# TensorE's and VectorE's order written out in the first stage of a two-layer encoder kernel, and the input's high part taken straight from x

## The chip, the cores and the metric

The kernel runs on one core of a Trainium2 chip. The metric is the device time of one execution in microseconds; the time before is the median of three executions.

## The reference

Two layers over a sequence of 512 tokens of width 1024, batch 1, in float32. Layer 0 mixes tokens by stick-breaking attention with 16 heads, layer 1 by a gated token-mixing MLP; each mixer is followed by a SwiGLU feed-forward part. Every part has an adaptive norm in front, and the change is in the first of these and the projections behind it:

```python
shift, scale, gate = jnp.split(silu(c) @ w_ada + b_ada, 3, axis=-1)
h = rms_norm(x, g) * (1.0 + scale) + shift          # (512, 1024)
qkv = h @ w_qkv                                     # (512, 3072)
...                                                 # attention on q, k, v
x = x + gate * rms_norm(y, post_g)
```

## The kernel before

All matmuls that carry the result run as three products of float32r parts: a tensor is split into a high part (a rounding copy on ScalarE) and a low part (its difference on VectorE), and `mm3` issues high x high, high x low and low x high. Weight tiles of 512 KB stream through `wload` (the load, two raw buffers) and `wemit` (the split `wh`, `wl`, five buffers); `wget` asks for a tile and may run ahead.

The first stage normalizes x (`norm0`), transposes it to eight column blocks `xhT` of 128 features by 512 tokens (`turn0`), and needs per feature a scale `Ac = (1 + scale) * g` and a shift `Bc`, as columns. The adaLN product for them is taken in five blocks: for features 0 to 255 in two rows (`row0`, on TensorE), for the rest in three blocks of 512 columns (`ada0_sum`): eight multiply-add steps on VectorE (`ada_stt`) into `acc`, then four one-column matmuls (`cols0`, output `ab`) that sum over the partitions. `h0` forms `Ac` and `Bc` on VectorE, scales `xhT` in place on ScalarE, and splits it into `hTh` and `hTl`. A step k of the projections uses one column block: `v_step` has 12 matmuls into four banks (first half of v), `qk0_step` has 6 into `pq` and `pk` (first pair of heads). Blocks b = 1, 2, 3 of the adaLN columns belong to k = 2 and 3, 4 and 5, 6 and 7.

Behind it come the second half of v, the attention with the other q and k projections between its parts (`fill`), and the adaLN gate of layer 0 (`Bg`: VectorE steps `G`, `A`, `B` over loads `rawada`, summed over partitions by matmuls with `ones` into a bank that the attention scores call z).

A scheduler puts the instructions in each engine's queue, in order of their readiness by its own costs. Where a chain is on (`pe["chain"]`, `Vector.chain`), TensorE's or VectorE's instructions keep the order in which the program writes them. Before, both chains are off in the first stage and come on in the attention. Loads are issued by SP in one queue, at most eight in flight before it waits for an earlier one to land. ScalarE has no chain.

Of the kernel before, what the change touches and what calls it, by code (L numbers as in the profile page):

```python
# [31 lines left out]
def trunk(ctx: ExitStack, tc: tile.TileContext, A: dict, out: bass.AP):  # L32
    nc = tc.nc

    consts = ctx.enter_context(tc.tile_pool(name="consts", bufs=1))
    wraw = ctx.enter_context(tc.tile_pool(name="wraw", bufs=2))
    wpool = ctx.enter_context(tc.tile_pool(name="wpool", bufs=5))
    adas = ctx.enter_context(tc.tile_pool(name="adas", bufs=1))
# [10 lines left out]
    def nm(s):  # L49
        uid[0] += 1  # L50
        return f"{s}_{uid[0]}"
# [4 lines left out]
    def bank(name, tag="b"):  # L56
        return psum.tile([P, 512], F32, tag=tag, bufs=6 if tag == "b" else 2, name=nm(name))

    act = nc.scalar
    pe = {"prev": None, "chain": False}  # L60

    class Vector:


        chain, prev = False, None

        def __getattr__(self, op):
            def call(*args, **kw):
# [16 lines left out]
    def order(b, before):  # L85
        tc.add_manual_dep(
            b.ins, before.ins.name,
            mybir.DependencyInfo(mybir.DependencyClass.NoSync, mybir.DependencyReason.DATA),
            reason="order",
        )  # L90

    def mm(o, l, r, start, stop, after=None):
        b = nc.tensor.matmul(o, l, r, start=start, stop=stop, skip_group_check=True)  # L93
        pe_op(b)
        if after is not None:
            order(b, after)
# [15 lines left out]
    def split(hi, lo, src, hi_dve=False):  # L112
        if hi_dve:
            dve.tensor_copy(hi, src)
        else:
            act.activation(hi, src, AF.Copy)  # L116
        dve.tensor_tensor(lo, src, hi.bitcast(F32), ALU.subtract)
# [19 lines left out]
    def wemit():  # L137
        n = len(got)
        src, a, b, key = stream[n]
        if len(raws) == n:  # L140
            wload()
        if src is None:
            if len(raws) == n + 1 < len(stream) and stream[n + 1][0] is None:
                wload()
            got.append(blocks(*raws[n]))
            return
        raw = raws[n]
        if key[0] == "wdn" and key[2] in SEVEN[key[1]]:
            got.append(down_blocks(raw))
            return  # L150
        h, l = wtile(a, b)
        if key[0] == "wqk" and key[1]:

            act.activation(h[:], raw[:], AF.Copy)
            nc.vector.tensor_tensor(l[:], raw[:], h[:].bitcast(F32), ALU.subtract)
            if len(raws) == n + 1 and stream[n + 1][3][0] == "wqk":
                wload()
        else:
            act.activation(h[:], raw[:], AF.Copy)  # L159
            nc.vector.tensor_tensor(l[:], raw[:], h[:].bitcast(F32), ALU.subtract)  # L160
        got.append((h, l))

    def wtile(a, b):
# [121 lines left out]
    def ada0_raw(b, q):  # L285

        nk, n = (4, 256) if b < 2 else (2, 512)
        raw = stp.tile([P, nk, n], F32, tag="ra", bufs=8, name=nm("ada0"))
        load(raw[:], A["ada0s"][b, q] if b < 2 else A["ada0p"][b - 2, q])
        return raw  # L290

# [37 lines left out]
    class Bg:  # L329
# [79 lines left out]
    def hTk(hT, k, lo, n):  # L409
        h, l = hT[k // 2]  # L410
        return h[:, k % 2, lo : lo + n], l[:, k % 2, lo : lo + n]
# [162 lines left out]
        bg.step(bg0.step(n))  # L574


    b1 = consts.tile([P, KD], F32, name="b1")
    dve.tensor_scalar(b1[:], cols[:, 0, :], 1.0, None, ALU.add)

    xhT = [slot(F32, "xhT") for _ in range(4)]  # L580

# [37 lines left out]

    onec = oneb[:, 0:1]  # L620

    def ada0_sum(raws, n, nk, tag="acch"):
        acc = adas.tile([P, 512], F32, tag=tag, name=nm("acc"))
        nc.gpsimd.memset(acc[:, :n], 0.0)
        for q, raw in enumerate(raws):
            for k in range(nk):
                ada_stt(acc[:, :n], raw[:, k, :], q * nk + k)
        return acc

    def cols0(acc, n):  # L630

        ps = bank("ab0", "p")
        for i in range(n):
            mm(ps[:, i : i + 1], acc[:, i * P : (i + 1) * P], onec, True, True)
        return ps

    def row0(raws):

        ps = bank("ab0", "p")
        for q, raw in enumerate(raws):  # L640
# [3 lines left out]
        dve.tensor_copy(row[0:1, :], ps[0:1, :256])  # L644
        ps = bank("ab0", "p")
        for i in range(2):
            mm(ps[:, i : i + 1], row[0:1, i * P : (i + 1) * P], oneb[0:1, 0:1], True, True)
        return ps

    def h0(ps, i, k):  # L650

        Ac = small.tile([P, 1], F32, tag="Ac", name=nm("Ac"))
        Bc = small.tile([P, 1], F32, tag="Bc", name=nm("Bc"))
        dve.tensor_scalar(
            Ac[:], ps[:, i : i + 1], b1[:, k : k + 1], cols[:, 2, k : k + 1], ALU.add, ALU.mult
        )
        dve.tensor_scalar(Bc[:], ps[:, i + 1 : i + 2], cols[:, 1, k : k + 1], None, ALU.add)
        xk = xhT[k // 2][:, k % 2, :]
        act.activation(xk, xk, AF.Identity, scale=Ac[:], bias=Bc[:])
# [11 lines left out]
    norm0(1)  # L671
    turn0(0)
    norm0(2)
    ab0 = row0(a0)
    turn0(1)
    norm0(3)
    turn0(2)
    turn0(3)
    wv0.append(wget(("wv", 0, 0), 0))
    a2 = [ada0_raw(2, q) for q in range(4)]  # L680
    h0(ab0, 0, 0)
    ab1 = row0(a1)
    wqk0.append(wget(("wqk", 0, 0), 0))
    vb = [bank("v0") for _ in range(NT)]
    pq0, pk0 = bank("pq"), bank("pk")
    v_step(vb, 0, 0, wv0[0])
    h0(ab1, 0, 1)
    wqk0.append(wget(("wqk", 0, 1), 0))
    wload()
    acc = ada0_sum(a2, 512, 2)  # L690
    for b in range(1, 4):

        if b > 1:
            v_step(vb, 0, 2 * b - 2, wv0[b - 1])
        qk0_step(2 * b - 2)
        an = [ada0_raw(b + 2, q) for q in range(4)] if b < 3 else []
        if b == 1:
            v_step(vb, 0, 1, wv0[0])
        ps = cols0(acc, 4)
        h0(ps, 0, 2 * b)  # L700
        wv0.append(wget(("wv", 0, b), 0))
        h0(ps, 2, 2 * b + 1)
        if b < 3:
            wload()
            acc = ada0_sum(an, 512, 2, ("acch", "accl")[b % 2])
        if b > 1:
            v_step(vb, 0, 2 * b - 1, wv0[b - 1])
        if b == 2:
            bg0.step(3)
        qk0_step(2 * b - 1)  # L710
        if b == 3:
            bg0.step(1)
    for k in (6, 7):
        v_step(vb, 0, k, wv0[3])
        bg0.step(1)
        qk0_step(k)
        bg0.step(1)
# [758 lines left out]
```

## Time and profile before

| | us |
|---|---|
| median of three executions | 1159.36 (1157.38 to 1160.34) |
| the profiled execution, whole | 1159.46 |
| its span, first to last instruction | 1157.7 |
| mean granted TensorE clock | 0.996 |

Times in the views count from the span's start. In rows of instructions the first number is the start and the second the duration; in brackets stands the engine's idle time before it and what ended it. PE is TensorE, DVE VectorE, ACT ScalarE, POOL GpSimd, SP SyncE, which issues the loads. A 128x512 row of `v` is one matmul of the first stage. Lines are those of the kernel before; most rows carry the line of a helper (L93 is `mm`, L69 is `Vector`, L116 is `split`).

### The profile page before, as it was taken

To read this page: it belongs to the slowest core of one execution; us is meant where nothing else is said; L and a number is where in the kernel's file an instruction comes from. 1 tells how busy PE (TensorE), PEld (TensorE's weight loads), DVE (VectorE), ACT (ScalarE), POOL (GpSimd) and SP (SyncE) were. 2 spreads that over 40 slices of the span, in tenths; PEclk is the share of its full clock that TensorE was granted. 3 is DMA by queue.
4 is the path that set the end of the run, shared out by engine and by line. 5 is a ranking of instruction groups with operands and counts; after the bars stand their busy time and mean duration, and the time that the engine had idled before them with its cause. 6 is when DMAs were issued, how large, how long until landed. Compare 5 with 4: busy or idle time off the path is not lost.

```text
span 1157.7 us, 18780 instructions
## 1 busy us (share of the span) xinstructions
PE 1133.7 (98%) x7526; PEld 1011.6 (87%) x7526; DVE 943.4 (81%) x1220; ACT 587.6 (51%) x977; POOL 23.8 (2%) x43
## 2 busy tenths in 40 slices
PE   6999999999999999999999999999999999999997
PEld 4777888878999999998887898988999999999996
DVE  4987999875998998878686965668979898889996
ACT  6344454555665555554142633526545555565752
POOL 0020000000000000000000100000000000000000
PEclk9999999999999999999999999999999999999999
DMA  8764334213424444338887374224243433223242
GB/s 310 279 240 158 128 110 128 91 56 127 162 93 142 137 141 137 121 114 276 279 279 246 135 248 170 91 74 164 93 145 128 159 132 127 78 90 97 89 149 104
DMA packets 50811, 174.43 MB, mean 151 GB/s; under 512 B 5786, under 2 KB 9114, under 8 KB 50724
## 3 DMA queue, kind: packets, MB, share of 16 engines
q1 hardware_dynamic: 48996, 166.94, 42.6%
q0 software_dynamic: 1728, 6.29, 1.4%
q8 instruction: 59, 0.97, 0.3%
q14 instruction: 28, 0.23, 0.1%
HBM read 164.82 MB, written 8.39 MB: 150 GB/s over the span
## 4 chain that ended last, share of the span: by engine, by line
PE 87%; DVE 5%; DMA 3%; ACT 2%; issue 1%; SPq 0%; DVEq 0%; ACTq 0%
PE r L93 31%; PE y L93 15%; PE pqk L93 7%; PE v L93 6%; PE gu L93 5%; PE X L93 4%; PE Y L93 3%; PE u L93 3%; PE av L93 3%; PE z L93 2%; PE Z L93 1%; PE W L93 1%; PE tw L101 1%; PE tp L101 1%; PE ab L93 1%
## 5 line engine op out<-in xcount | busy, mean ns | idle before, releaser
L93 PE MATMUL r<-Sh,wl 128*128 128x256 f32 x608 | 170.3, 280 | 0.0
L93 PE MATMUL r<-Sh,wh 128*128 128x256 f32 x608 | 170.1, 280 | 0.0
L93 PE MATMUL r<-Sl,wh 128*128 128x256 f32 x608 | 170.0, 280 | 0.0
L93 PE MATMUL y<-wh,as 128*128 128x512 f32 x480 | 153.1, 396 | 0.4 <-DVE G L69 0.4
L159 ACT ACTIVATE wh<-raw 128x1024 fp32r<-128x1024 f32 x87 | 91.6, 1058 | 115.2 <-PE y L93 62.1
L69 DVE TENSOR_TENSOR wl<-f,wh 128x1024 fp32r<-128x1024 f32 x87 | 106.1, 1219 | 38.9 <-ACT wh L116 38.8
L116 ACT ACTIVATE wh<-f 128x1024 fp32r<-128x1024 f32 x87 | 92.3, 1061 | 89.0 <-PE r L93 66.2
L160 DVE TENSOR_TENSOR wl<-raw,wh 128x1024 fp32r<-128x1024 f32 x87 | 105.7, 1219 | 38.6 <-ACT wh L159 38.3
L93 PEld LDWEIGHTS r<-Sh,wh 128*128 128x128 f32 x608 | 114.6, 189 | 0.2 <-ACT e L1033 0.2
L93 PEld LDWEIGHTS r<-Sl,wh 128*128 128x128 f32 x608 | 114.5, 188 | 0.0
L93 PEld LDWEIGHTS r<-Sh,wl 128*128 128x128 f32 x608 | 114.5, 188 | 0.0
L93 PEld LDWEIGHTS y<-wh,as 128*128 128x128 f32 x480 | 90.1, 188 | 21.7 <-DVE G L69 0.8
L93 PE MATMUL y<-wl,as 128*128 128x512 f32 x240 | 94.9, 395 | 0.0
L93 PE MATMUL r<-hTh,wh 128*128 128x256 f32 x304 | 89.1, 293 | 0.3 <-DVE gu L69 0.2
L93 PE MATMUL r<-hTl,wh 128*128 128x256 f32 x304 | 84.9, 280 | 0.0
L93 PE MATMUL r<-hTh,wl 128*128 128x256 f32 x304 | 80.1, 280 | 0.0
L93 PEld LDWEIGHTS r<-hTh,wh 128*128 128x128 f32 x304 | 57.2, 188 | 6.1 <-DVE gu L69 1.9
L93 PE MATMUL r<-hTh,b 128*128 128x256 f32 x304 | 60.7, 282 | 0.0
L93 PEld LDWEIGHTS r<-hTl,wh 128*128 128x128 f32 x304 | 57.4, 189 | 0.1
L116 ACT ACTIVATE wh<-rawx 128x1024 fp32r<-128x1024 f32 x38 | 40.4, 1062 | 32.3 <-PE r L93 30.9
L93 PE MATMUL v<-wh,hTh 128*128 128x512 f32 x128 | 52.2, 408 | 3.1 <-ACT hTh L116 3.1
L93 PEld LDWEIGHTS r<-hTh,wl 128*128 128x128 f32 x304 | 55.2, 189 | 0.0
(261 smaller groups left out, 3023.8 us busy)
## 6 DMA issues: line engine op xcount, KB each, us to landing
rawada<-in_ada SPq DMA_DIRECT2D x80, 512.0 KB, 4.6
rawy<-in_wy SPq DMA_DIRECT2D x38, 512.0 KB, 3.5
rawx<-in_wx SPq DMA_DIRECT2D x38, 512.0 KB, 4.4
raw<-in_wdown SPq DMA_DIRECT2D x22, 512.0 KB, 4.5
raw<-in_wdn SPq DMA_DIRECT2D x22, 512.0 KB, 3.6
raw<-in_wqk SPq DMA_DIRECT2D x16, 512.0 KB, 4.5
ada<-in_ada0p SPq DMA_DIRECT2D x12, 512.0 KB, 6.0
raw<-in_wgu SPq DMA_DIRECT2D x12, 512.0 KB, 3.6
```

The lines of the kernel that those rows point to most:

```text
L69: b = getattr(nc.vector, op)(*args, **kw)
L93: b = nc.tensor.matmul(o, l, r, start=start, stop=stop, skip_group_check=True)
L101: last_tp[0] = nc.tensor.transpose(o, i, ident)
L116: act.activation(hi, src, AF.Copy)
L159: act.activation(h[:], raw[:], AF.Copy)
L160: nc.vector.tensor_tensor(l[:], raw[:], h[:].bitcast(F32), ALU.subtract)
```

## The change

- TensorE's and VectorE's chains are on from the first h step to the end of the first half of v, and weight tiles split in that time put their low part into VectorE's chain too (`dve.weights`). ScalarE's two activations of `h0` keep their order among themselves; its weight passes are left to the scheduler.
- The steps are written in another order: `v_two` issues the eight matmuls with h's high part first and the four with its low part last; the column sums (`sums0`) stand ahead of the q and k matmuls of the block's last k; the eight `ada_stt` steps are dealt out between the low parts (`Sum0.step`).
- `h0` computes h's high part from x in one scaled activation, then x itself by a second one; the low part is their difference.
- The constants (1 + bias, bias) enter the column sums as one more matmul with the identity (`cols0`), and one VectorE multiplication gives scale and shift of two k.
- Eleven buffers instead of eight for the adaLN loads of the stage; two of the second block's four loads are issued ahead of a weight tile's.
- The adaLN gate's steps in the stage are placed anew (3, 1, 1, then 3 instead of 3, 1, 1, 1, 1, 1).

In the queues as built, ScalarE's rows from the first column sums on stand thus (k in brackets):

```
before: wh(wqk 1) wh(wv 1) | x(2) h(2) x(3) h(3) wh(wv 2) | x(4) x(5) h(4) h(5) wh(wv 3)
after:  wh(wqk 1) | h(2) x(2) h(3) wh(wv 1) x(3) wh(wv 2) | h(4) x(4) h(5) wh(wv 3) x(5)
```

On SP the load of wv's sixth tile (second half of v, second tile) stands behind the attention's mask loads, before it stood ahead of five adaLN loads and the masks. From about the 260th row of TensorE's queue and the 120th of VectorE's on, the queues of both kernels hold the same order.

```diff
-            nc.vector.tensor_tensor(l[:], raw[:], h[:].bitcast(F32), ALU.subtract)
+            (dve if dve.weights else nc.vector).tensor_tensor(
+                l[:], raw[:], h[:].bitcast(F32), ALU.subtract
+            )
...
-        raw = stp.tile([P, nk, n], F32, tag="ra", bufs=8, name=nm("ada0"))
+        raw = stp.tile([P, nk, n], F32, tag="ra", bufs=11, name=nm("ada0"))
...
-    def cols0(acc, n):
+    def cols0(k):
         ps = bank("ab0", "p")
-        for i in range(n):
-            mm(ps[:, i : i + 1], acc[:, i * P : (i + 1) * P], onec, True, True)
+        mm(ps[:, 0:4], ident, add[:, k : k + 2, :].rearrange("p n a -> p (n a)"), True, False)
         return ps
+    def sums0(ps, acc, k):
+        for i in range(4):
+            mm(ps[:, i : i + 1], acc[:, i * P : (i + 1) * P], onec, False, i == 3)
+        ab = small.tile([P, 2, 2], F32, tag="ab", name=nm("ab"))
+        dve.tensor_tensor(
+            ab[:], ps[:, :4].rearrange("p (n a) -> p n a", a=2), mul[:, k : k + 2, :], ALU.mult
+        )
+        return ab
...
-    def h0(ps, i, k):
+    def h0(ab, i, k):
...
-        act.activation(xk, xk, AF.Identity, scale=Ac[:], bias=Bc[:])
         h, l = hTk(hT, k, 0, T)
-        split(h, l, xk)
+        for o in (h, xk):
+            b = act.activation(o, xk, AF.Identity, scale=ab[:, i, 0:1], bias=ab[:, i, 1:2])
+            if h0_last[0] is not None:
+                order(b, h0_last[0])
+            h0_last[0] = b
+        dve.tensor_tensor(l, xk, h.bitcast(F32), ALU.subtract)
...
+    def v_two(k, w, between=None):
+        for tt in range(NT):
+            a, b = hTk(hT, k, tt * P, P)
+            for i in range(2):
+                mm(vb[tt][:], a, w[i][:, k % 2, :], k + i == 0, False)
+            if between and tt == 1:
+                between()
+        for tt in range(NT):
+            a, b = hTk(hT, k, tt * P, P)
+            mm(vb[tt][:], b, w[0][:, k % 2, :], False, k == KD - 1)
...
+    dve.chain = dve.weights = pe["chain"] = True
...
     for b in range(1, 4):
-        if b > 1:
-            v_step(vb, 0, 2 * b - 2, wv0[b - 1])
-        qk0_step(2 * b - 2)
-        an = [ada0_raw(b + 2, q) for q in range(4)] if b < 3 else []
-        if b == 1:
-            v_step(vb, 0, 1, wv0[0])
-        ps = cols0(acc, 4)
-        h0(ps, 0, 2 * b)
-        wv0.append(wget(("wv", 0, b), 0))
-        h0(ps, 2, 2 * b + 1)
+        ps = cols0(2 * b)
+        if b == 1:
+            wqk0.append(wget(("wqk", 0, 1), 0))
+        else:
+            v_two(2 * b - 2, wv0[b - 1])
+            qk0_step(2 * b - 2)
+            v_two(2 * b - 1, wv0[b - 1])
+            wv0.append(wget(("wv", 0, b), 0))
+        ab = sums0(ps, acc.acc, 2 * b)
+        if b == 1:
+            wv0.append(wget(("wv", 0, b), 0))
+            qk0_one(0, 1)
+            qk0_one(1, 1)
+        else:
+            qk0_step(2 * b - 1)
         if b < 3:
+            raws0[b + 1] = raws0.get(b + 1) or [ada0_raw(b + 2, q) for q in range(4)]
+            acc = Sum0(raws0[b + 1], ("acch", "accl")[b % 2])
+            if b == 2:
+                acc.step(2)
+            h0(ab, 0, 2 * b)
+            acc.step(1)
+            h0(ab, 1, 2 * b + 1)
             wload()
...
+    dve.chain = dve.weights = pe["chain"] = False
+    bg0.step(3)
```

More of the change, by code (lines that the diff above doesn't have):

```diff
@@ L65, in trunk @@
         chain, prev = False, None
+        weights = False
         def __getattr__(self, op):
@@ L574, in ada_step @@
         bg.step(bg0.step(n))
-    b1 = consts.tile([P, KD], F32, name="b1")
-    dve.tensor_scalar(b1[:], cols[:, 0, :], 1.0, None, ALU.add)
+    add = consts.tile([P, KD, 2], F32, name="add")
+    dve.tensor_copy(add[:, :, 1], cols[:, 1, :])
+    dve.tensor_scalar(add[:, :, 0], cols[:, 0, :], 1.0, None, ALU.add)
+    mul = consts.tile([P, KD, 2], F32, name="mul")
+    dve.memset(mul[:, :, 1], 1.0)
+    dve.tensor_copy(mul[:, :, 0], cols[:, 2, :])
     xhT = [slot(F32, "xhT") for _ in range(4)]
@@ L620, in trunk, with __init__, step @@
     onec = oneb[:, 0:1]
[L622 to L628, printed above, removed]
-    def cols0(acc, n):
+    class Sum0:
+        def __init__(self, raws, tag):
+            self.acc = adas.tile([P, 512], F32, tag=tag, name=nm("acc"))
+            nc.gpsimd.memset(self.acc[:], 0.0)
+            self.todo = [(raw[:, k, :], 2 * q + k) for q, raw in enumerate(raws) for k in range(2)]
+        def step(self, n=8):
+            for _ in range(min(n, len(self.todo))):
+                ada_stt(self.acc[:], *self.todo.pop(0))
+    def cols0(k):
         ps = bank("ab0", "p")
-        for i in range(n):
-            mm(ps[:, i : i + 1], acc[:, i * P : (i + 1) * P], onec, True, True)
-        return ps
+        mm(ps[:, 0:4], ident, add[:, k : k + 2, :].rearrange("p n a -> p (n a)"), True, False)
+        return ps
+    def sums0(ps, acc, k):
[6 more added lines that the diff above has]
+        return ab
     def row0(raws):
@@ L644, in row0, with row_cols @@
         dve.tensor_copy(row[0:1, :], ps[0:1, :256])
+        return row
+    def row_cols(row):
         ps = bank("ab0", "p")
@@ L648, in row0, with scales @@
         return ps
-    def h0(ps, i, k):
[L652 to L657, printed above, removed]
+    def scales(ps, k):
+        ab = small.tile([P, 2, 2], F32, tag="ab", name=nm("ab"))
+        dve.tensor_tensor(ab[:, 0, :], ps[:, :2], add[:, k, :], ALU.add)
+        dve.tensor_tensor(ab[:, 0, :], ab[:, 0, :], mul[:, k, :], ALU.mult)
+        return ab
+    h0_last = [None]
+    def h0(ab, i, k):
         xk = xhT[k // 2][:, k % 2, :]
-        act.activation(xk, xk, AF.Identity, scale=Ac[:], bias=Bc[:])
         h, l = hTk(hT, k, 0, T)
-        split(h, l, xk)
+        for o in (h, xk):
[4 more added lines that the diff above has]
+        dve.tensor_tensor(l, xk, h.bitcast(F32), ALU.subtract)
     wv0, wqk0 = [], []
@@ L673, in trunk @@
     norm0(2)
-    ab0 = row0(a0)
+    ab0 = row_cols(row0(a0))
     turn0(1)
@@ L679, in trunk, with qk0_one @@
     wv0.append(wget(("wv", 0, 0), 0))
-    a2 = [ada0_raw(2, q) for q in range(4)]
-    h0(ab0, 0, 0)
-    ab1 = row0(a1)
+    def qk0_one(k, e):
+        h, l = hTk(hT, k, 0, T)
+        w, pb = wqk0[e], (pq0, pk0)[e]
+        mm3(pb[:], w[0][:, k, :], w[1][:, k, :], h, l, k == 0, k == KD - 1)
+    def v_two(k, w, between=None):
[8 more added lines that the diff above has]
+            mm(vb[tt][:], b, w[0][:, k % 2, :], False, k == KD - 1)
+    raws0 = {1: [ada0_raw(2, q) for q in range(4)]}
+    dve.chain = dve.weights = pe["chain"] = True
+    h0(scales(ab0, 0), 0, 0)
+    row1 = row0(a1)
     wqk0.append(wget(("wqk", 0, 0), 0))
@@ L685, in trunk @@
     pq0, pk0 = bank("pq"), bank("pk")
-    v_step(vb, 0, 0, wv0[0])
+    ab1 = []
+    v_two(0, wv0[0], lambda: ab1.append(row_cols(row1)))
+    acc = Sum0(raws0[1], "acch")
+    ab1 = scales(ab1[0], 1)
+    acc.step(2)
     h0(ab1, 0, 1)
-    wqk0.append(wget(("wqk", 0, 1), 0))
+    qk0_one(0, 0)
     wload()
-    acc = ada0_sum(a2, 512, 2)
+    raws0[2] = [ada0_raw(3, q) for q in range(2)]
+    wload()
+    raws0[2] += [ada0_raw(3, q) for q in range(2, 4)]
+    acc.step()
+    v_two(1, wv0[0])
@@ L691, in trunk @@
+    qk0_one(1, 0)
     for b in range(1, 4):
-        if b > 1:
-            v_step(vb, 0, 2 * b - 2, wv0[b - 1])
-        qk0_step(2 * b - 2)
-        an = [ada0_raw(b + 2, q) for q in range(4)] if b < 3 else []
+        ps = cols0(2 * b)
         if b == 1:
-            v_step(vb, 0, 1, wv0[0])
-        ps = cols0(acc, 4)
-        h0(ps, 0, 2 * b)
-        wv0.append(wget(("wv", 0, b), 0))
-        h0(ps, 2, 2 * b + 1)
-        if b < 3:
-            wload()
-            acc = ada0_sum(an, 512, 2, ("acch", "accl")[b % 2])
@@ L706, in trunk @@
[L706 to L711, printed above, removed]
+            wqk0.append(wget(("wqk", 0, 1), 0))
[11 more added lines that the diff above has]
+            qk0_step(2 * b - 1)
@@ L712, in trunk @@
+        if b < 3:
+            raws0[b + 1] = raws0.get(b + 1) or [ada0_raw(b + 2, q) for q in range(4)]
+            acc = Sum0(raws0[b + 1], ("acch", "accl")[b % 2])
+            if b == 2:
+                acc.step(2)
+            h0(ab, 0, 2 * b)
+            acc.step(1)
+            h0(ab, 1, 2 * b + 1)
+            wload()
+            acc.step()
+            if b == 2:
+                bg0.step(3)
+        else:
             bg0.step(1)
+            h0(ab, 0, 6)
+            bg0.step(1)
+            h0(ab, 1, 7)
@@ L713, in trunk @@
     for k in (6, 7):
-        v_step(vb, 0, k, wv0[3])
-        bg0.step(1)
+        v_two(k, wv0[3])
         qk0_step(k)
-        bg0.step(1)
+    dve.chain = dve.weights = pe["chain"] = False
+    bg0.step(3)
     cc = stp.tile([P, P], F32, name="cc")
```

## Prediction

> **What bounds the kernel now.** I read the page first (span, busy shares, chain), then the windows of the stage that is edited, then the rows of each engine in order of time.
>
> ```profile
> span 1157.7 us, 18780 instructions
> PE 1133.7 (98%) x7526; PEld 1011.6 (87%) x7526; DVE 943.4 (81%) x1220; ACT 587.6 (51%) x977; POOL 23.8 (2%) x43
> PE 87%; DVE 5%; DMA 3%; ACT 2%; issue 1%; SPq 0%; DVEq 0%; ACTq 0%
> ...
> 23.90:35.90 12.00, 10.94 (x49) 7.90 (x48) 11.09 (x20) 4.79 (x7) 1.42 (x2) 1.00 0.68 241
> 35.90:46.80 10.90, 10.84 (x44) 8.70 (x44) 9.08 (x16) 3.10 (x5) 0.00 (x0) 0.85 0.98 378
> ...
> 32.40:35.80 3.40, 2.63 (x14) 1.64 (x12) 3.39 (x8) 1.34 (x2) 1.42 (x2) 1.00 0.54 172
> 35.80:39.20 3.40, 3.24 (x8) 2.58 (x9) 3.37 (x7) 2.57 (x4) 0.00 (x0) 0.50 0.93 319
> 39.20:42.60 3.40, 3.40 (x16) 2.77 (x15) 3.26 (x5) 0.00 (x0) 0.00 (x0) 1.00 1.00 394
> ```
>
> TensorE is busy 98% of the span; all that any edit can remove of its idle time is 1157.7 - 1133.7 = 24 us. The edit touches the stage from the first v matmul (23.9 us) to the second half of v (67.3 us). In the windows (columns: length, PE, PEld, DVE, ACT, POOL busy, granted clock, DMA share, GB/s) VectorE is as full there as TensorE: 11.09 of 12.00 us. And from 35.8 to 39.2 us the granted clock is 0.50, after a window in which TensorE was busy 2.63 of 3.40 us.
>
> ```profile
> 23.88 0.50 PE L93 MATMUL v<-wh,hTh 128*128 128x512 f32 x1
> 35.96 0.80 PE L93 MATMUL v<-wh,hTh 128*128 128x512 f32 x1 [0.74 <-ACT hTh L116]
> 36.55 0.63 PE L93 MATMUL v<-wl,hTh 128*128 128x512 f32 x1
> 36.98 0.63 PE L93 MATMUL v<-wh,hTh 128*128 128x512 f32 x1
> 44.75 0.95 PE L93 MATMUL ab<-oneb,acc 128*128 128x1 f32 x8
> 45.88 0.39 PE L93 MATMUL pq<-hTh,wl 128*128 128x512 f32 x1
> 48.27 0.50 PE L93 MATMUL v<-wh,hTh 128*128 128x512 f32 x1 [1.30 <-ACT hTh L116]
> 48.61 0.39 PE L93 MATMUL v<-wl,hTh 128*128 128x512 f32 x1
> 48.84 0.39 PE L93 MATMUL v<-wh,hTh 128*128 128x512 f32 x1
> 58.64 0.50 PE L93 MATMUL v<-wh,hTh 128*128 128x512 f32 x1 [0.84 <-ACT hTh L116]
> 67.30 0.50 PE L93 MATMUL v<-wh,hTh 128*128 128x512 f32 x1
> ```
>
> A 512-wide matmul takes 48.84 - 48.61 = 0.23 us at full clock and 36.98 - 36.55 = 0.43 us at half. One group of adaLN column sums (four, eight records) costs 45.88 - 44.75 - 0.23 = 0.9 us. The waits that the edit is aimed at are the three before k = 2, 4, 6: 0.74 + 1.30 + 0.84 = 2.9 us, all ended by ScalarE's h high part.
>
> ```profile
> 28.40 2.00 ACT L159 ACTIVATE wh<-raw 128x1024 fp32r<-128x1024 f32 x2
> 34.42 0.82 ACT L659 ACTIVATE xhT<-xhT,Bc,Ac 128x512 f32<-128x512 f32 x1 [4.03 <-DVE Bc L69]
> 46.17 1.52 ACT L659 ACTIVATE xhT<-xhT,Bc,Ac 128x512 f32<-128x512 f32 x2 [7.50 <-DVE Bc L69]
> 47.60 1.13 ACT L116 ACTIVATE hTh<-xhT 128x512 fp32r<-128x512 f32 x2
> 6.43 0.16 DVE L69 RECIPROCAL r<-sd 128x1 f32<-128x1 f32 x1 [0.92 <-ACT sd L400]
> 24.80 0.40 DVE L69 COPY row<-ab 1x256 f32<-1x256 f32 x1
> 29.73 3.11 DVE L69 SCALAR_TENSOR_TENSOR acc<-ada,sc,acc 128x512 f32<-128x512 f32 x4
> 32.76 1.22 DVE L160 TENSOR_TENSOR wl<-raw,wh 128x1024 fp32r<-128x1024 f32 x1
> 33.99 0.28 DVE L69 TENSOR_SCALAR Ac<-ab,b,cols 128x1 f32<-128x1 f32 x1
> 36.41 0.69 DVE L69 TENSOR_TENSOR hTl<-xhT,hTh 128x512 fp32r<-128x512 f32 x1
> ```
>
> **The change, part by part.** *h from x.* Before, the high part comes after two dependent ScalarE passes and, for k = 4 and 6, after both k of the pair: 47.60 + 1.13/2 - 46.17 = 2.0 us. After, it is one scaled pass of 0.82 us (taken from the x pass; the copy's 1.13/2 is the lower bound), so 1.2 us earlier. x follows it, and h's low part waits for x.
>
> *Constants in TensorE's sums.* Four Ac/Bc operations of about 0.2 to 0.28 us become one of 0.28; TensorE gets three matmuls of four columns, at most 0.9/4 = 0.2 to 0.3 us each, placed where it has no other work or against 0.7 us of VectorE. Three more tiny operations at the start lie in the 0.92 us before VectorE's first reciprocal: nothing.
>
> *Eleven buffers.* They let SP issue two loads of the next block before the load that waits for VectorE's split of the first wqk tile. No wait of the sums on these loads stands in VectorE's rows, so nothing.
>
> *The written order.* This decides. I walk it with the durations above, on the trace's clock.
>
> Block 1: the row sum is done at 23.9. VectorE then does the row copy 0.4, a weight's low part 1.2, two ab operations 0.5, two sum steps 1.6, waits 0.3 for x of k = 1, h's low part 0.6, six sum steps of 3.11/4 = 0.78, 4.7: the sums are ready at 33.2 (before: 29.73 + 3.11 = 32.84). TensorE's sums end at 34.1; VectorE finishes the low part of the second wqk tile (1.2) at 34.4 and ab at 34.7; ScalarE has h of k = 2 at 35.5, and TensorE has by then done the six q and k matmuls that were moved behind the sums (34.1 + 1.4 + 0.3 = 35.8). So far the wait of 0.74 is gone.
>
> But in ScalarE's queue, as the changed kernel is built, the next rows are h(2), x(2), h(3), and only then the high part of the weight tile wv 1, which before stood ahead of the h rows (second of the pair at 28.40). Nothing pins ScalarE's weight passes, and its queue runs in order. So: h(2) 34.7 to 35.5, x(2) to 36.4, h(3) to 37.1, wh (2.00/2 and its tail) to 38.0. The first v matmul of k = 2 starts at 38.0 instead of 35.96. VectorE, now in the written order, has that tile's low part ahead of everything: 38.0 to 39.2, and the second matmul starts at 39.25, with h's low parts and all eight sum steps of block 2 queued behind it.
>
> Block 2: VectorE from 39.1: 2 x 0.6 + 8 x 0.78 = 7.5, sums ready at 46.6. TensorE has 29 matmuls, 6.8 us: 46.0 at full clock. An idle stretch longer than the 0.74 us before 35.96 (35.8 to 39.25 with one matmul in it) lets me expect the half clock again, for one window of 3.4 us: 3.4/0.43 = 8 matmuls, then 21 x 0.23: 47.5. Sums to 48.4, six matmuls and the constants 1.7: k = 4 starts at 50.1 (49.2 at full clock; before 48.27).
>
> Block 3: VectorE has ab at 48.8, two steps, h's low part at 50.5 (x(4) is just done), one step, then waits until 52.9 for x(5), which stands behind wv 3 on ScalarE; low part 0.6 and five steps 3.9: 57.4. TensorE arrives with 30 matmuls at 57.1. Sums to 58.4, six matmuls: k = 6 at 59.8 (59.05 at full clock; before 58.64). Then 36 matmuls, 8.4 us, and at most 0.3 for h's low part: the second half of v starts at 68.3 (67.6 at full clock) against 67.30: **+1.0 us (+0.3)**.
>
> After that the built queues hold the same order as before from about 95 us on, and TensorE's 36.0 of 36.0 us between 94 and 130 carries the shift to the end. Between them:
>
> ```profile
> 84.96 4.79 DMA raw<-in_wqk
> 92.04 0.40 PE L93 MATMUL v<-wh,hTl 128*128 128x512 f32 x1
> 92.09 0.68 DVE L69 TENSOR_TENSOR G<-z,g 128x512 f32<-128x512 f32 x1
> 92.92 0.47 PE L93 MATMUL z<-acch,ones 128*128 128x512 f32 x1 [0.49 <-ACT Vh L116]
> 93.43 0.50 PE L93 MATMUL z<-accl,ones 128*128 128x512 f32 x1
> 93.76 0.40 PE L93 MATMUL pqk<-hTh,wh 128*128 128x512 f32 x1
> 94.00:130.00 36.00, 36.00 (x199) 28.72 (x198) 31.34 (x32) 14.16 (x27) 0.95 (x1) 1.00 0.47 154
> ```
>
> Two matmuls of the adaLN gate (z from acch, accl) wait for G on VectorE (92.09), which stands behind the low part of the fourth wqk tile, which waits for a load (84.96 + 4.79 = 89.75). Without it the first would stand near 92.27, 0.23 behind its predecessor at 92.04: it and its partner cost 93.76 - 92.27 - 2 x 0.23 = 1.0 us. In the changed queue G stands behind the third wqk tile instead. That one I get at VectorE's end near 91.3 (wv 2's low part at 76.9, load 4.8, split 1.1 + 1.2 at 84.2, again load 4.8 and split), G at 92.0, and TensorE comes at 92.9: **-1.0 us**, with 0.9 us of margin; if the margin goes, 0.
>
> Sum: +1.0 - 1.0 = 0.0 us on the profiled execution's 1159.46 us (span 1157.7 and 1.8 around it), which is 0.1 above the median of 1159.36. **Forecast: no change, 1159.4 us.**
>
> **The rivals.** *The clock holds* (a little faster). If the stretch before k = 2's second matmul does not halve the clock, the walk's full-clock figures stand: +0.3 - 1.0 = -0.7, 1158.7 us. For it: one matmul breaks the stretch, and at 48.27 the clock held after 1.30 us of idle time. Against: it fell after 35.8 although TensorE had been busy 2.63 of the 3.40 us before. [...]
>
> *The waits go as meant* (faster). If wv 1's high part were ready by 35.8, k = 2 would start there, the clock would hold, VectorE would finish block 2's sums near 43.3, k = 4 would start near 45.9, k = 6 near 55.4, the second half of v near 63.9: -3.4, and with the gate's 1.0 up to -4.4: 1155 to 1156 us. For it: the raw tile has landed by 29.4 (second wh of 28.40). Against: the queue's order.
>
> *The clock stays at half* (slower). Place: the run of 29 matmuls from 39.25. Each further half-clock window costs 3.4/2 = 1.7 us of TensorE's time, of which the 0.6 us that VectorE is later hides little. Two windows give +1.7: 1161.2; three give +3.4, 1162.9; it is over 0.3% from three windows on.
>
> ```profile
> 7.44 1.97 PE L101 MATMUL tp<-identt,x 128*128 128x128 f32 x8 [7.44 <-DVE x L69]
> 18.98 1.42 PE L101 MATMUL tp<-identt,x 128*128 128x128 f32 x11
> 60.36 5.96 SPq L110 DMA_DIRECT2D ones<-in_consts  x8
> raw<-in_wv SPq DMA_DIRECT2D x8, 512.0 KB, 6.9
> ```
>
> For it: the first transposes take 1.97/8 = 0.25 us against 1.42/11 = 0.13 later, so a start with gaps can stay slow. Against: after 39.2 the clock was back after one dense window.
>
> *A late second-half tile* (slower). The load of wv's sixth tile, which before was issued ahead of the attention masks' eight small loads, is moved behind them and four adaLN loads. They start after the last sum step (57.4) and a memset of about 1. Eight took 5.96 us, waits included; twelve at 0.45 (without waits, an estimate below that row) to 0.75 each end at 64 to 67.4. With the 4.8 of 84.96 to the 6.9 us of the wv group it lands between 69 and 74.3; its split, behind adaLN steps, must end when TensorE asks: 68.3 + 24 x 0.23 and the score matmuls, 75.2. From a landing later than about 72 each us is one us; at the far end +2.3, 1161.7.
>
> **How the numbers follow.** A measurement of this kernel can tell about 0.3% (3.5 us) from no change. Forecast with its bounds (0 to +1.0 where the gate's wait stays): 0.52. Clock holds: 0.15. Waits as meant: 0.08. Clock at half for two windows 0.06, for three or more 0.06. Late tile: 0.09. Unknown: 0.04, shared. Faster by over 0.3%: 0.08 and half the unknown, 0.10. Slower by over 0.3%: three windows, the other half, and the late tile together with a long half clock, 0.12. Same: 0.78. The range goes from 1156.9 (full clock, 1158.7, less half of the way to the faster case) to 1162.0 (two windows, 1161.2, or the late tile, 1161.7, with a little of the other).
>
> **What would show it.** Right: an idle stretch before k = 2's v ended by ScalarE's wh (line 160), about 2 us, then one of about 1 us ended by VectorE's wl; no wait over 0.5 us ended by hTh; a clock of 0.50 for one window after it; the second half of v starting 67 to 69 us; the gate's wait near 92 gone. Wrong: k = 2 starting by 36 us (the faster case), a clock of 0.50 past 46 us, or a wait on wv tiles after 70 us.

## The result, and the profile after

The changed kernel takes 1161.81 us (median of 15 executions, 1159.24 to 1163.31), the kernel before 1159.08 in the same session (15 executions, 1157.07 to 1161.52). The ratio is 1.0022, with a 95% interval from 1.0014 to 1.0030: a small loss of about 2.7 us, inside the range of the prediction (1156.9 to 1162.0) and 2.4 us above its value of 1159.4. The profiled execution of the changed kernel took 1161.96 us.

Its page, with the span, the busy shares and the chain of waits:

```profile
span 1160.2 us, 18779 instructions
PE 1136.4 (98%) x7532; PEld 1016.2 (88%) x7532; DVE 942.9 (81%) x1214; ACT 589.4 (51%) x977; POOL 23.8 (2%) x43
PE 87%; DVE 6%; DMA 3%; ACT 2%; issue 1%; SPq 0%; POOL 0%; DVEq 0%; POOLq 0%; ACTq 0%
```

TensorE is busy 2.7 us longer than before (1136.4 against 1133.7), the span is 2.5 us longer, and so the loss is not idle time. TensorE's rows of the changed kernel, in order of time, at the places that the prediction walks through:

```profile
22.67 0.49 PE L94 MATMUL v<-wh,hTh 128*128 128x512 f32 x1
36.53 0.80 PE L94 MATMUL v<-wh,hTh 128*128 128x512 f32 x1 [1.84 <-ACT wh L160]
37.78 0.79 PE L94 MATMUL v<-wl,hTh 128*128 128x512 f32 x1 [0.46 <-DVE wl L70]
48.55 0.48 PE L94 MATMUL v<-wh,hTh 128*128 128x512 f32 x1
58.35 0.39 PE L94 MATMUL v<-wh,hTh 128*128 128x512 f32 x1
67.92 0.50 PE L94 MATMUL v<-wh,hTh 128*128 128x512 f32 x1 [0.91 <-DVE Vl L70]
92.88 0.40 PE L94 MATMUL z<-acch,ones 128*128 128x512 f32 x1
93.35 0.39 PE L94 MATMUL pqk<-hTh,wh 128*128 128x512 f32 x1
1152.04 0.40 PE L94 MATMUL Y<-wh,al 128*128 128x512 f32 x1
```

The last matmul of the kernel before:

```profile
1149.66 0.40 PE L93 MATMUL Y<-wh,al 128*128 128x512 f32 x1
```

Cut at these rows, the 2.38 us between the last matmuls are the sum of four pieces, each the difference of two rows:

| piece | before | after | difference |
|---|---|---|---|
| span's start to the first v matmul | 23.88 | 22.67 | -1.21 |
| first v matmul to the second half of v | 43.42 | 45.25 | +1.83 |
| second half of v to the first pqk matmul | 26.46 | 25.43 | -1.03 |
| first pqk matmul to the last matmul | 1055.90 | 1058.69 | +2.79 |

The first piece lies ahead of the change, but for three tiny VectorE operations, and differs from execution to execution: the start of v lies between 22.37 and 24.32 us in the profiles of three builds of the kernel before that differ in an unused tile, two buffers or one idle instruction (below). The second and third piece are what the prediction worked out. The fourth is the surprise: 2.79 us in a part in which both queues hold the same instructions in the same order. It isn't a wait that came in somewhere: matmul by matmul the distance between the two kernels grows over the whole piece, by 0.4 us in each 150 us on average. Two matmuls that are the same in both kernels, the first `r` and the first `X` of the last feed-forward part, have 1588 matmul starts between them. Before:

```profile
841.04 0.28 PE L93 MATMUL r<-hTh,wh 128*128 128x256 f32 x1
1031.77 0.39 PE L93 MATMUL X<-wh,ah 128*128 128x512 f32 x1
```

After:

```profile
842.59 0.28 PE L94 MATMUL r<-hTh,wh 128*128 128x256 f32 x1
1033.69 0.39 PE L94 MATMUL X<-wh,ah 128*128 128x512 f32 x1
```

190.73 us have become 191.10. Taken over all pairs of neighbouring matmuls of one width and 128 rows behind 100 us whose starts are less than 0.27 us apart, the pitch (start to start) of 256-wide matmuls rose from 119.64 to 120.17 ns, that of 512-wide ones from 232.70 to 233.09. The granted clock is 1.00 there in both.

### The profile page after: what moved, and what is told of

It is laid out like the page before. It is cut to its first block, busy times and chain, and to the rows that moved or that the text cites. A ratio compares the mean times of both kernels' runs of the same rounds, so it can differ in the third digit from the quotient of the medians.

```text
span 1160.2 us, 18779 instructions
## 1 busy us (share of the span) xinstructions
PE 1136.4 (98%) x7532; PEld 1016.2 (88%) x7532; DVE 942.9 (81%) x1214; ACT 589.4 (51%) x977; POOL 23.8 (2%) x43
## 4 chain that ended last, share of the span: by engine, by line
PE 87%; DVE 6%; DMA 3%; ACT 2%; issue 1%; SPq 0%; POOL 0%; DVEq 0%; POOLq 0%; ACTq 0%
PE r L94 32%; PE y L94 15%; PE pqk L94 7%; PE v L94 7%; PE gu L94 5%; PE X L94 4%; PE Y L94 3%; PE u L94 3%; PE av L94 3%; PE z L94 2%; PE W L94 1%; PE Z L94 1%; PE tw L102 1%; DMA rawada<-in_ada 1%; PE sv L94 1%
## 5 line engine op out<-in xcount | busy, mean ns | idle before, releaser
L161 DVE TENSOR_TENSOR wl<-raw,wh 128x1024 fp32r<-128x1024 f32 x82 | 99.7, 1219 | 39.8 <-ACT wh L160 39.3
L70 DVE TENSOR_TENSOR_SCAN left<-ga,ones 128x1027 f32<-128x1027 f32 (+2 forms) x24 | 46.4, 1934 | 10.5 <-ACT ga L915 10.5
```

Of the source, the lines that this page charges most:

```text
L70: b = getattr(nc.vector, op)(*args, **kw)
L161: (dve if dve.weights else nc.vector).tensor_tensor(l[:], raw[:], h[:].bitcast(F32), ALU.subtract)
```

## The experiments

Two questions: does the stage lose its time where the prediction says, at one weight pass in ScalarE's queue; and why did TensorE's pace change? Each kernel ran 6 to 12 times (most 11 or 12) on the same chip as the kernel before; the ratios in brackets are to that kernel, with their 95% intervals. Differences to the changed kernel compare medians of different sessions.

**Addresses as such.** The two new constants `add` and `mul` take 64 bytes each where `b1` took 32, and the four buffers of `ab` take 128 bytes where those of `Ac` and `Bc` took 256. So, as the builder places them, the weights lie 96 bytes higher and the activations 32 bytes lower than before, which swaps their remainders of 64 bytes. An unused tile of 32 bytes at the front swaps them in the kernel before, and swaps them back in the changed one.

```diff
+    pad = consts.tile([P, 8], F32, name="pad")
+    nc.gpsimd.memset(pad[:], 0.0)
     cT = consts.tile([P, KD], F32, name="cT")
```

> The kernel before with one unused 32-byte tile ahead of all others in on-chip memory: every later tile lies 32 bytes higher, which puts weights and moving operands on the remainders of 64 bytes that they have in the changed kernel; nothing else differs. Theory A (TensorE's pace hangs on where its operands lie): the pace of the changed kernel appears here, 0.5 ns more per 256-wide and 0.4 ns more per 512-wide matmul, spread evenly; over the whole span about +2.8 us, near 1162. Theory B (the two profiled executions differed in pace by chance): no change of the times, 1159.1 within 0.4.

> The changed kernel with the same unused 32 bytes: weights and moving operands are back on the remainders of the kernel before. Theory A (addresses): about 2.8 us less than the changed kernel, near 1159.0, and so no more than the kernel before, since the rest of the change cancels (the stage up to the second half of v later by under 2, the adaLN gate's wait gone); pitch of 512-wide matmuls 232.7 ns. Theory B (chance, and the change itself costs 2.7): no change against the changed kernel, 1161.8.

Measured: the kernel before with the tile 1157.45 us (ratio to the kernel before 0.9989, 0.9979 to 1.0000), pitch 119.68 and 232.73 ns; the changed kernel with it 1161.95 (1.0027, 1.0016 to 1.0038), 120.12 and 233.10 ns. So theory A fell in both directions, and B fell too: the pace came back the same in new executions, each kernel with its own.

**ScalarE's weight pass.** The place that the prediction names, undone: one instruction moves ahead by three places.

```diff
-            act.activation(h[:], raw[:], AF.Copy)
+            c = act.activation(h[:], raw[:], AF.Copy)
+            if dve.weights and key == ("wv", 0, 1):
+                h0_last[0] = c
```

> The changed kernel with ScalarE's high part of the second wv tile put ahead of h of k = 2 in ScalarE's queue (one instruction moves by three places). If that place is what costs the stage: k = 2's v starts near 34.6 us instead of 36.5 and 37.8, no half clock after it, VectorE's sums of block 2 end near 42.2, the second half of v starts near 65 instead of 67.9, and the total is about 2.9 us lower than the changed kernel's, near 1158.9. Rival (the clock halves anyway, or the wait for VectorE's sums takes the place): second half of v at 67 or later, less than 1 us gained, 1161.

Measured: 1158.47 us (ratio 1.0000, 0.9989 to 1.0011), 3.3 less than the changed kernel. ScalarE's row of that pass, and TensorE's rows:

```profile
29.48 1.06 ACT L160 ACTIVATE wh<-raw 128x1024 fp32r<-128x1024 f32 x1 [1.54 <-DMA raw<-in_wv]
```

```profile
34.91 0.48 PE L94 MATMUL v<-wh,hTh 128*128 128x512 f32 x1
35.23 0.39 PE L94 MATMUL v<-wl,hTh 128*128 128x512 f32 x1
43.05 1.05 PE L94 MATMUL ab<-oneb,acc 128*128 128x1 f32 x8 [0.89 <-DVE acc L70]
65.00 0.40 PE L94 MATMUL v<-wh,hTh 128*128 128x512 f32 x1
```

The window that holds k = 2 (length, PE, PEld, DVE, ACT, POOL, granted clock, DMA share, GB/s):

```profile
34.90:38.30 3.40, 3.40 (x18) 2.76 (x17) 2.71 (x4) 3.01 (x4) 0.01 (x1) 1.00 0.95 352
```

Both waits of k = 2 are gone, the clock stays at 1.00 through k = 2, and the second half of v starts at 65.00 as expected. The rival's other wait is there, but small: 0.89 us before the next column sums. One window of half clock came all the same, later (45.3 to 48.7 us), behind that wait. The pitch is still the slow one (120.18 ns).

**The gate's steps.** The changed kernel's VectorE waits 1.51 us for a gate load ahead of Vl, which holds up the second half of v. Here the last three gate steps come behind the conversion of v (the order of some loads on SP and of some of ScalarE's passes changes with them).

```diff
     dve.chain = dve.weights = pe["chain"] = False
-    bg0.step(3)
...
     v_evac(vb, 0)
+    bg0.step(3)
```

> The changed kernel with the last three gate steps issued behind the conversion of v instead of ahead of it. If VectorE's wait for a gate load ahead of Vl is what delays the second half of v by 0.9 us: that wait (1.5 us before G, then 0.9 before v) is gone, the second half starts near 67.0, and the total is about 0.9 lower, 1160.9. Rival (something later takes it back, such as the gate's wait near 92 us): no change, 1161.8.

Measured: 1162.67 us (1.0040, 1.0025 to 1.0054), no gain.

```profile
67.30 0.40 PE L94 MATMUL v<-wh,hTh 128*128 128x512 f32 x1
73.51 0.29 PE L94 MATMUL z<-k,q 64*128 64x128 f32 x1 [0.44 <-DVE q L70]
74.01 1.12 PE L94 MATMUL z<-k,q 64*128 64x128 f32 x11 [0.21 <-DVE k L70]
93.66 0.39 PE L94 MATMUL pqk<-hTh,wh 128*128 128x512 f32 x1
```

The wait ahead of the second half of v is gone, and the total is the rival's: VectorE pays later, with q and k of the first pair (0.44 and 0.21 us), and the first pqk matmul comes hardly earlier (70.5 us behind the first v matmul, against 70.7). But that the edit took the wait away isn't shown, for it comes and goes without it. The changed kernel with the unused front tile has the same order in the queues of TensorE, VectorE, ScalarE and SP, and in its profile the three gate steps run on without a wait and TensorE goes straight into the second half of v:

```profile
62.99 3.92 DVE L70 SCALAR_TENSOR_TENSOR G<-rawada,sc,G 128x1024 f32<-128x1024 f32 x3
67.97 0.39 PE L94 MATMUL v<-wh,hTh 128*128 128x512 f32 x1
```

The wait is missing with the drain (below) too, and is 0.47 us long with the unused tile of 128 bytes (below). That the median lies 0.9 us above the changed kernel's, while the profiled execution (1161.57) does not, no row explains.

**Position in TensorE's queue.** The changed kernel's matmuls lie an odd number of instructions later in the queue than before. One drain at its head, where nothing is to be waited for, makes the shift even.

```diff
+    for _ in range(1):
+        nc.tensor.drain()
     turn0(0)
```

> The changed kernel with one more instruction (a drain that waits for nothing, since TensorE has no work yet) at the head of TensorE's queue. Behind 105 us the changed kernel's matmuls stand 11 (from 304 us on 9) instructions later in that queue than the same matmuls of the kernel before: three more sums with 4 instructions each, and 1 and then 3 waiting instructions fewer; the shift is odd. With the drain it is even. Theory P (the pace hangs on where a matmul's pair of instructions lies in TensorE's stream, even or odd): the pace of the kernel before comes back, 119.65 ns per 256-wide and 232.7 per 512-wide matmul, and the time falls by about 2.5 us, to 1159.3. Rival (the pace belongs to something else of the change): 120.15 and 233.1 ns, 1161.8.

> The kernel before with the same drain at the head of TensorE's queue, and nothing else. Theory P: every matmul is moved by one instruction, the pace is that of the changed kernel, 120.15 and 233.1 ns, and the time rises by about 2.5 us to 1161.5. Rival: no change of pace or time, 1159.

> The changed kernel with both repairs: ScalarE's high part of the second wv tile ahead of h of k = 2, and the drain at the head of TensorE's queue. If the two are independent and theory P holds, 1158.5 less 2.5, about 1156.0, the first version ahead of the kernel before by about 0.25%. Rival (P wrong): 1158.5.

Measured: the changed kernel 1163.05 us (1.0035, 1.0019 to 1.0050), pitch 120.31 ns, with a second half-clock window near 821 us in the profiled execution; the kernel before 1158.85 (0.9998, 0.9980 to 1.0015), 119.62 ns; with both repairs 1158.91 (0.9995, 0.9981 to 1.0010), 120.14 ns. Theory P fell three times: each kernel kept its pace.

**The written order taken away.** The other three parts stay.

```diff
-    dve.chain = dve.weights = pe["chain"] = True
```

> The changed kernel without the written order of TensorE and VectorE: h from x, the constants in TensorE's sums and eleven buffers stay, and the scheduler places the instructions as it does in the kernel before. It puts q and k of k = 2 ahead of v of k = 2, so that ScalarE's late high part of the second wv tile has cover. Behind 105 us its matmuls stand 10 instructions later than those of the kernel before, an even shift. If the written order is what costs the stage, the second half of v starts at 66 to 67 instead of 67.9; with theory P the pace is the fast one (119.65 ns), and the total lies near 1158. If the order is neutral and P is wrong: 1161.8.

Measured: 1167.09 us (1.0078, 1.0051 to 1.0105), 5.3 more than with the order, and neither theory's number. TensorE's rows at the end of the first half, then the loads on SP and ScalarE's pass:

```profile
62.52 0.40 PE L94 MATMUL pk<-hTh,wl 128*128 128x512 f32 x1
69.48 0.79 PE L94 MATMUL v<-wh,hTh 128*128 128x512 f32 x1 [6.56 <-ACT wh L160]
```

```profile
57.43 3.65 SPq L111 DMA_DIRECT2D ones<-in_consts  x8
61.12 0.90 SPq L111 DMA_DIRECT2D raw<-in_wv  x2
```

```profile
68.39 1.99 ACT L160 ACTIVATE wh<-raw 128x1024 fp32r<-128x1024 f32 x2
```

The first half is done at 62.9, about 4 us ahead of the changed kernel (67.92 - 0.91 = 67.0), and then TensorE waits 6.56 us for the fifth wv tile, whose load the scheduler put behind the eight mask loads. The granted clock is at half from 65.45 to 75.69 us, over the wait and 6.2 us beyond it; the piece from the second half of v to the first pqk matmul takes 28.70 us, 3.3 more than in the changed kernel. So the written order, with its wait and its half clock, makes the first half about 4 us longer than the scheduler's, and the total is higher without it through this late load and the half clock behind it. The window in which the clock is still at half behind the wait (length, PE, PEld, DVE, ACT, POOL, granted clock, DMA share, GB/s), and the next:

```profile
72.28:75.69 3.41, 3.41 (x10) 2.64 (x9) 0.49 (x1) 1.06 (x1) 0.00 (x0) 0.50 0.86 293
75.69:79.10 3.41, 3.41 (x21) 2.59 (x21) 1.97 (x2) 1.06 (x1) 0.00 (x0) 1.00 0.97 356
```

This is the prediction's rival of a late second-half tile, on the tile before the one it named; in the changed kernel that load is issued at 46 us. The pitch is slow again (120.10 ns), with an even shift, which counts against P once more.

**The distance of weights and activations.** What all kernels with the change share and all without it lack: the activations lie 128 bytes nearer to the weights (96 up, 32 down). A front tile moves both alike and could not show this. In the kernel before, two buffers fewer for Ac and Bc bring the activations 128 bytes nearer; in the changed kernel an unused tile between them brings the distance back. The order of all other instructions stays.

```diff
# the kernel before
-        Ac = small.tile([P, 1], F32, tag="Ac", name=nm("Ac"))
-        Bc = small.tile([P, 1], F32, tag="Bc", name=nm("Bc"))
+        Ac = small.tile([P, 1], F32, tag="Ac", bufs=2, name=nm("Ac"))
+        Bc = small.tile([P, 1], F32, tag="Bc", bufs=2, name=nm("Bc"))
# the changed kernel
+    pad = small.tile([P, 32], F32, tag="pad", bufs=1, name="pad")
+    nc.gpsimd.memset(pad[:], 0.0)
```

> The kernel before with two buffers instead of four for the small columns Ac and Bc: the order of every engine's instructions is the same, but all activations (moving operands) lie 128 bytes lower against the weights, as they do in the changed kernel (weights up by 96, activations down by 32). Theory R (TensorE's pace hangs on the distance of moving and stationary operands in on-chip memory): pace of the changed kernel, 120.15 ns per 256-wide and 233.1 per 512-wide matmul, and about 2.5 us more, 1161.4. Rival (the pace comes with the changed stage itself, through something that no run has moved yet): 119.65 and 232.7 ns, 1158.9.

> The changed kernel with an unused tile of 128 bytes between weights and activations, which brings their distance back to that of the kernel before. Theory R: 119.65 and 232.7 ns and about 2.5 us less than the changed kernel, 1159.3. Rival: no change, 1161.8.

> The changed kernel with the second wv tile's high part ahead of h of k = 2 on ScalarE, and the same unused 128 bytes. Theory R: the 3.3 us that the first repair gave and about 2.5 more, 1156.0, ahead of the kernel before by 0.25%. Rival: 1158.5.

Measured: the kernel before, nearer, 1160.67 us (1.0017, 1.0005 to 1.0028), 120.14 and 233.11 ns; the changed kernel at the old distance 1159.48 (1.0002, 0.9992 to 1.0012), 119.66 and 232.77 ns; with ScalarE's pass ahead as well 1156.29 (0.9973, 0.9963 to 0.9982), 119.65 and 232.76 ns. The same pair of rows, in the kernel before with activations nearer:

```profile
841.93 0.28 PE L93 MATMUL r<-hTh,wh 128*128 128x256 f32 x1
1033.03 0.40 PE L93 MATMUL X<-wh,ah 128*128 128x512 f32 x1
```

and in the changed kernel at the old distance:

```profile
842.44 0.28 PE L94 MATMUL r<-hTh,wh 128*128 128x256 f32 x1
1033.14 0.40 PE L94 MATMUL X<-wh,ah 128*128 128x512 f32 x1
```

191.10 and 190.70 us: the two kernels have changed places. Theory R holds in both directions, in pace and in time (1.7 us more than the kernel before, where 2.5 were expected, and 2.3 less than the changed kernel), and the last kernel beats both, by 0.27% of the kernel before.

**Another distance.** The same kernel with 192 unused bytes instead of 128.

```diff
-    pad = small.tile([P, 32], F32, tag="pad", bufs=1, name="pad")
+    pad = small.tile([P, 48], F32, tag="pad", bufs=1, name="pad")
```

> The last kernel with 192 unused bytes instead of 128: the activations lie 64 bytes further from the weights than in the kernel before (the changed kernel: 128 bytes nearer). If only two classes of distance exist, 128 bytes apart, this one lies in the fast class (119.65 and 232.75 ns, 1156.3) or in the slow one (120.15 and 233.1 ns, 1158.5); a pace between the two, or a faster one, would mean that finer steps count.

Measured: 1160.60 us (1.0024, 1.0013 to 1.0036), 4.3 more for 64 bytes, and a third pace, 120.76 and 233.41 ns:

```profile
841.48 0.28 PE L94 MATMUL r<-hTh,wh 128*128 128x256 f32 x1
1033.61 0.40 PE L94 MATMUL X<-wh,ah 128*128 128x512 f32 x1
```

192.13 us. So finer steps than two classes count. All kernels together, by the distance of activations from weights against the kernel before (in the names, pad is the front tile, d1 the drain, wfirst ScalarE's pass put ahead, gate the gate's steps, nochain the order taken away, sm the 128 bytes, sm192 the 192):

| distance | kernels | pitch, 256-wide (ns) | first pqk matmul to the last matmul (us) |
|---|---|---|---|
| as before | before, before_pad, before_d1, after_sm, wfirst_sm | 119.62 to 119.68 | 1055.9 to 1057.5 |
| 128 bytes nearer | after, after_pad, after_wfirst, after_gate, after_d1, wfirst_d1, after_nochain, before_sm | 120.10 to 120.31 | 1058.0 to 1059.9; after_d1, with its second half-clock window, 1061.0 |
| 64 bytes further | wfirst_sm192 | 120.76 | 1060.9 |

The traces hold a control of their own. Not every pair of operands changed its distance: some matmuls read both from tiles that moved alike, such as `r` with the third matrix `b`. Pair by pair against the kernel before (neighbouring 256-wide matmuls whose starts are 100 to 135 ns apart, behind 100 us), the 1145 pairs whose operands moved alike are 0.1 ns slower in the changed kernel, 0.1 in before_sm and 0.2 in wfirst_sm192. The 2821 to 2825 pairs with the activation as moving operand and the weight as the stationary one, whose distance changed, are 0.8, 0.8 and 3.1 ns slower. Where the weight is the moving operand (349 pairs) it is 1.6, 1.6 and -0.5. For 512-wide matmuls no such line can be drawn: in the changed kernel it is 0.2 ns in 1133 pairs that changed their distance and 1.2 in 134 that didn't.

## Why the prediction was right, and where it was not

*The wait moves to ScalarE's weight pass, behind h(2) x(2) h(3).* Right, and the step that carries the stage. ScalarE's rows of the changed kernel:

```profile
33.16 0.82 ACT L688 ACTIVATE hTh<-xhT,ab 128x512 fp32r<-128x512 f32 x1 [5.72 <-DVE ab L70]
34.01 0.81 ACT L688 ACTIVATE xhT<-xhT,ab 128x512 f32<-128x512 f32 x1
34.73 0.80 ACT L688 ACTIVATE hTh<-xhT,ab 128x512 fp32r<-128x512 f32 x1
35.43 1.04 ACT L160 ACTIVATE wh<-raw 128x1024 fp32r<-128x1024 f32 x1
```

Counted from the first v matmul, since this execution started 1.21 us earlier: k = 2's first matmul forecast at 14.1 and measured at 13.9 us, its second at 15.4 and 15.1, k = 4 at 26.2 and 25.9, k = 6 at 35.9 and 35.7. The kernel with that one pass put ahead shows that it is the cause: 3.3 us.

*One window of half clock.* Half right. The windows of the changed kernel (length, PE, PEld, DVE, ACT, POOL, granted clock, DMA share, GB/s):

```profile
22.70:34.70 12.00, 10.89 (x53) 8.81 (x52) 9.70 (x15) 4.09 (x5) 1.42 (x2) 0.98 0.68 240
34.40:37.80 3.40, 1.10 (x5) 0.51 (x3) 1.29 (x2) 3.40 (x5) 0.01 (x1) 0.50 0.94 355
37.80:41.20 3.40, 3.40 (x8) 2.72 (x9) 3.33 (x6) 0.33 (x1) 0.00 (x0) 0.52 1.03 420
41.20:44.60 3.40, 3.40 (x16) 2.72 (x15) 3.26 (x5) 0.00 (x0) 0.00 (x0) 1.00 0.39 152
```

The clock was half for two windows, as in the rival, but the first of them lies over the wait itself; only the second, with 8 matmuls where the next has 16, costs time. So the forecast's price of one window was right for another reason here. With the same order, the profiles with the front tile, the drain and the 128 bytes have one half window behind the wait, as the walk has it (39.4 to 42.8 us with the front tile). The walk took the length of the idle stretch for what halves the clock; the last section has what the traces show of that.

*Second half of v +1.0 us.* In this execution +1.83. The walk held up to k = 6; what it lacked is the wait of 0.91 us ahead of the second half. VectorE's rows, and SP's:

```profile
65.98 1.28 DVE L70 SCALAR_TENSOR_TENSOR G<-rawada,sc,G 128x1024 f32<-128x1024 f32 x1 [1.51 <-DMA rawada<-in_ada]
67.18 2.48 DVE L70 TENSOR_TENSOR Vl<-v,Vh 128x512 fp32r<-128x512 f32 x4
```

```profile
59.25 3.21 SPq L111 DMA_DIRECT2D rawada<-in_ada  x4
```

The prediction saw four gate loads that are moved behind the mask loads, but asked only what they do to the weight tile behind them, not which VectorE step needs them. The load is not late each time: where the wait is missing (front tile, drain), the piece takes 44.25 and 44.24 us, +0.8 against the kernel before, close to the forecast. So the wait is a term with a chance, and one profile could not tell. The late wv tile itself, the rival, did not come: TensorE waits for no tile between 68 and 75 us.

*The gate's wait near 92 us, -1.0.* Right: z from acch and accl and the first pqk matmul follow each other at 92.88, 93.11 and 93.35, and the piece is 1.03 us shorter.

*"Carries the shift to the end."* This is the step that failed. Same order and full busy time were taken for same duration, and the 2.79 us of slower pace came on top. No term of the sum and no rival has it. That 1161.81 lies inside the range is luck: the upper end of 1162.0 was worked out from a second half-clock window that slows matmuls or a late weight tile, and neither came. Without the slower pace the forecast's own sum is near what is measured: at the old distance the changed kernel takes 1159.48 us, forecast 1159.4, ratio 1.0002 (in that profile the stage costs 1.4 us more than before and the gate's wait gives 1.0 back). The diff showed the two new constants and the columns that went, and their sizes were counted as no cost, while nobody asked what moves behind them.

*The clock holds* (rival, 0.15). The changed kernel's profile has two windows at half. In the kernel before it depends on the execution: of 105 executions beside the experiments, 36 have a mean granted clock of 0.998 or more, with a median of 1156.6 us, and 69 have 0.997 or less, with 1159.3; of the changed kernel's 15, none reaches 0.998. With ScalarE's pass put ahead, two of the four profiles (drain, 192 bytes) have no half window in the stage. The forecast took the window of the profiled execution for a fixed cost.

## What to carry to other kernels

Writing out the order of a full engine moved the wait here and didn't remove it: 0.74 us ahead of k = 2 behind ScalarE's h became 1.84 us behind its weight pass, which stands later in ScalarE's queue than before. So look for the instruction that nothing pins (here that weight pass), and for every load that changes its place ask which step reads it first. The wait for a gate load cost 0.91 us ahead of the second half of v in one execution and was missing with the front tile, in the same order: look at a second profile with the same order before an edit is made against a wait. When a difference grows evenly over a part in which nothing was changed (here from 119.64 to 120.17 ns per 256-wide matmul), compare the pitch of the same matmuls and the addresses of their operands before looking for a wait; an unused tile of 128 bytes between two pools is a cheap test, and here it was worth as much as the edit (2.3 us less than the changed kernel, where the edit cost 2.7).

## What the runs showed of the hardware

TensorE's pace behind 100 us went with the distance in on-chip memory between the region of the weights and the region of the activations: 119.62 to 119.68 ns per 256-wide matmul in the 5 kernels with the distance of the kernel before, 120.10 to 120.31 in the 8 with the activations 128 bytes nearer, and 120.76 in the one with 64 bytes further. With both regions moved together by 32 bytes it was 119.68 ns against 119.64 of the kernel before, and 120.12 against 120.17 of the changed one. The difference is there too in the stretches in which neither VectorE nor ScalarE was busy from one start to the next: the pitch (between 100 and 135 ns) was 117.3 ns before (157 pairs) and 118.6 after (166). The pattern changes with it: in a dense run of 512-wide matmuls the starts are apart by 232 and 235 ns in turn before, and by 231, 238 and 231 ns after. What makes the pace differ no run shows, and other distances were not tried.

In the clock records of the profiles before and after, the granted clock keeps one value for 20.48, 3.41 and 1112.75 us, and for 20.48, 6.83 and 1116.16 us: 6, 1 and 326, and 6, 2 and 327 times 3.413 us. It fell behind windows of that length with TensorE busy 2.64 us by the records (before, 32.39 to 35.80) or 2.38 (after, 30.84 to 34.25), and not behind ones with 2.12 (before, 46.04 to 49.46) or 2.02 (after, 1150.41 to 1153.83); the two behind which it fell hold one-column sums, the others do not. So in these profiles the records' busy time does not tell when it fell. A count of columns parts the windows of these two profiles: add up the columns of all matmul records that start in a window, 512 for a 512-wide one and 1 for a one-column sum. Behind 21 us, the windows at full clock that were followed by half clock hold 2568 columns (before) and 3080 (after), and at the kernels' end 2560 (before, 1148.55 to 1151.96) and none (after, behind the last matmul); every other one at full clock holds at least 3968 (before) and 3584 (after), where a dense window has about 7500 (an estimate: 3.41/0.2327 x 512). No kernel was made to test this, so it is a count in two profiles and no condition for the clock.
